# A decoder step on one core: the up products of the second MLP from seven block products in place of eight, in three of its four quarters, with sums of weights made in the first MLP

## The chip, the core and the metric

The kernel is one program on one core of a Trainium2 chip. TensorE (PE, its weight loads as PEld), VectorE (DVE), ScalarE (ACT), GpSimd (POOL) and SyncE (SP) run side by side, each through its own queue in order, and wait for each other on semaphores. The metric is device time of one execution in microseconds (us). Three runs of the kernel before are shown, and one more execution was profiled.

## What is computed

The reference is one step of a two-layer decoder over 512 prompt rows and 8 sample rows, 520 in all, width 1024. A pooling mixer, a first MLP, a sparse attention and a second MLP follow each other. The part that the change rewrites is the MLP, which both layers run with their own weights:

```python
D_MODEL = 1024
D_FF = 4 * D_MODEL

def rmsnorm(x, g):
    xf = x.astype(jnp.float32)
    y = xf * lax.rsqrt(jnp.mean(xf * xf, axis=-1, keepdims=True) + RMS_EPS)
    return (y * g.astype(jnp.float32)).astype(x.dtype)

def sq_relu_mlp(h, g, w_up, w_down):
    a = jax.nn.relu(rmsnorm(h, g) @ w_up)
    return (a * a) @ w_down
```

`w_up` is 1024 x 4096, `w_down` 4096 x 1024, all in 32-bit floats.

## The kernel before, in words

Everything is kept with the features on the 128 partitions: the residual `h` is 8 tiles (`CT`) of 128 x 520, and a weight unit is a 128 x 8 x 128 block, 512 KB: 8 tiles along the contraction for 128 output features. To keep the precision of 32 bits on TensorE, each operand is split into a high part (`hi`, a copy rounded to fp32r, made on ACT) and a low part (`lo`, the rest, made on DVE by a subtraction, `lo_of`, L200). A product is the sum of three: hi x hi, hi x lo, lo x hi. `gemm` (L231) therefore issues for a unit 8 tiles x 3 products x 2 halves of the 520 columns (`NH` = 260), which is 48 matmuls of 128 x 260.

An MLP (`mlp_jobs`, L695) goes in four quarters. A quarter has 8 up units (`up_post`, L705: evacuation from PSUM with relu and the norm on DVE, square on ACT, square and low part on DVE, into one of the tiles `at`) and then 8 down units that contract those 8 tiles and add into `h` (`down_post`, L716). The last down quarter of the second MLP (`last_quarter`, L745) goes by column halves, so that the first half's final norm runs beside the second half's products. In the first MLP (layer 0), between units, jobs of the compressed attention branch are filled in, by a table of 64 numbers (`FILLERS`, L42).

The order on every engine is written out by hand: `run` (L244) goes through a list of jobs. A job has loads (issued on SP's queue as `room` allows), a preparation (`prep`: the split of its weights, emitted two prepared jobs ahead), its matmuls (`pe`) and steps after them (`post`; the nth list entry is emitted n jobs later). A raw weight block lands in one of three buffers `wraw`; its split lands in one of two pairs `whi`, `wlo`. PSUM has two `mm` tiles and two `aux` tiles for the products. POOL issues no DMA in the first MLP and does nothing in the second but one multiplication at its end.

These lines carry most of it:

```python
for k, (xh, xl) in enumerate(xs):
    for wt, x in ((w.hi, xh), (w.hi, xl), (w.lo, xh)):
        for i in cols:
            TE.matmul(ps[0:m, i, 0:NH], wt[:, koff + k, 0:m], x[:, i * NH:(i + 1) * NH], ...

self.raw = wp.tile([P, 8, 128], F32, name="wraw", bufs=3)
nc.sync.dma_start(self.raw[:, 0:self.kt, 0:self.m], self.src)
```

Of the kernel before, what the change touches and what calls it, by code (L numbers as in the profile page):

```python
# [10 lines left out]
OP = mybir.AluOpType  # L11
# [127 lines left out]
class Job:  # L139
# [2 lines left out]

    after = None
# [6 lines left out]
def trunk(tc, a, o):  # L152
# [23 lines left out]
    hsave = pool("hd", space=bass.MemoryType.DRAM).tile([P, CT, NT], F32, name="hsave")  # L176
# [67 lines left out]
    def run(js, ahead=1, done=0):  # L244

        n = len(js)
        queue = {k: [(i, f) for i, j in enumerate(js) for c, f in j.loads if c == k] for k in room}
        issued = {k: 0 for k in room}

        def pump():  # L250
            for k in room:
                q = queue[k]
                while issued[k] < len(q) and room[k] > 0:
                    q[issued[k]][1]()
                    issued[k] += 1
                    room[k] -= 1

        with_prep = [i for i, j in enumerate(js) if j.prep]
        bars = [i for i, j in enumerate(js) if j.bar]

        def preps(i):

            nonlocal done
            while bars and bars[0] <= i:
                bars.pop(0)
            due = ahead - sum(k > i for k in with_prep[:done])
            for k in with_prep[done:done + due]:
                if bars and k > bars[0]:
                    break
                js[k].prep()  # L270
                done += 1
                for c, m in js[k].free_prep.items():
                    room[c] += m
                pump()

        late = {}
        pump()
        preps(-1)
        for i in range(n + 8):
# [10 lines left out]
            pump()  # L290
            if j.pe:
# [37 lines left out]
    def norm_job(emit=lambda: None):  # L329
        box = {}  # L330

        def pe():
            for i in range(2):
                box[i] = st["aux"]()
                TE.matmul(box[i][:, 0:NH], onesm, accn[:, i * NH:(i + 1) * NH], start=True, stop=True)  # L335

        def post():
            inv_rms(box)
            emit()

        return Job(pe=pe, post=post)
# [353 lines left out]
    def mlp_jobs(l, filler, done, before=lambda: None):  # L695
        ap, kind = {}, "w2" if l else "w"

        def open_a():
            ap["p"] = pool("ap")
            if l:  # L700
                pool("wz")

        at = {}

# [18 lines left out]
        js = []  # L723
        for q in range(4):
            for f in range(8):
                js.append(gemm_job(W(a["up"][l, 8 * q + f]), xpairs, up_post(8 * q + f), kind=kind))
                if not l and q in (1, 2):
                    js[-1].after = lambda x=("wink", "winv")[q - 1], b=f: S.dma_start(o[x][b], a_in[x][b])
                if q == f == 0:
                    js[-1].post.insert(0, None)  # L730
                    js[-1].after = lambda: (before(), open_a())
                    js.append(norm_job())
                js += filler()
            for ct in range(CT):
                xs = (lambda q=q: [(at[8 * q + k][:, 0], at[8 * q + k][:, 1]) for k in range(8)])
                if l and q == 3:
                    continue
                js.append(gemm_job(W(a["down"][l, q, ct]), xs, down_post(q, ct), kind=kind))
                js += filler()
        if l:  # L740
            js += last_quarter(xs)
        js.append(Job(hook=lambda: close(*["wz"] * l, "ap")))
        return js

    def last_quarter(xs):  # L745
# [1205 lines left out]
```

## Time and profile before

| what | value |
|---|---|
| three runs | 1391.57, 1390.76, 1391.56 us, median 1391.56 |
| the profiled execution | 1392.16 us, its span 1390.0 us |
| PE busy | 1345.2 us, 97% of the span, 10827 matmuls |
| PEld busy | 1261.3 us, 91% |
| DVE busy | 836.7 us, 60% |
| ACT busy | 570.8 us, 41% |
| POOL busy | 190.3 us, 14% |
| DMA | 189.52 MB, mean 136 GB/s |

The first MLP lies between about 150 and 590 us of the span, the second between about 1009 us and the end. A busy PE only says that matmuls overlap in the records: how long a unit takes is read from the distance between steps that follow each unit. An engine's idle time is listed with what ended it, and counts only where somebody waits for that engine.

### The profile page before, as it was taken

What the parts mean: (1) busy time and instruction counts of PE and PEld (TensorE: products, weight loads), DVE (VectorE), ACT (ScalarE), POOL (GpSimd) and SP (SyncE); (2) the same over time, 40 slices, a digit from 0 to 9 for tenths busy, and PEclk for the clock granted to TensorE, in tenths of its full rate; (3) what the DMA queues carried; (4) which work ended last, traced back from release to release, by engine and by line L of the source; (5) the groups of instructions that cost most, each with busy time, mean ns of one, the idle gap of its engine ahead of it and who ended that gap; (6) DMA issues with size and microseconds to landing.
All of it is one profiled execution on the core that took longest, in us unless ns stands there. A gap on an engine that the chain in (4) does not pass through costs nothing. (4 is left out here: it accounts for less than half of the span.)

```text
span 1390.0 us, 27557 instructions
## 1 busy us (share of the span) xinstructions
PE 1345.2 (97%) x10827; PEld 1261.3 (91%) x10827; DVE 836.7 (60%) x1307; ACT 570.8 (41%) x1012; POOL 190.3 (14%) x265
## 2 busy tenths in 40 slices
PE   7999999999999999999998999998999999999997
PEld 6788999999999999989996777667999999999996
DVE  2788766565565476556878887554554353453563
ACT  3655443333333243464445677563432222221231
POOL 0000000000000000012455764751000000000000
PEclk9999999999999999999999999999999999999999
DMA  7755244554455232339505675766223233322321
GB/s 261 224 153 185 77 136 137 167 165 139 139 172 161 76 107 77 98 131 231 142 26 177 187 207 185 215 204 193 92 87 94 91 94 95 96 92 91 92 91 62
DMA packets 110554, 189.52 MB, mean 136 GB/s; under 512 B 13641, under 2 KB 81482, under 8 KB 109786
## 3 DMA queue, kind: packets, MB, share of 16 engines
q1 hardware_dynamic: 102202, 166.65, 38.6%
q0 software_dynamic: 7168, 12.21, 3.6%
q10 hardware_dynamic: 1056, 8.92, 1.9%
q8 instruction: 85, 1.39, 0.4%
q14 instruction: 43, 0.35, 0.1%
HBM read 177.59 MB, written 16.43 MB: 140 GB/s over the span
## 5 line engine op out<-in xcount | busy, mean ns | idle before, releaser
L237 PE MATMUL mm<-xn,whi 128*128 128x260 f32 (+1 forms) x2784 | 450.0, 284 | 0.4 <-DVE xn L201 0.3
L237 PEld LDWEIGHTS mm<-xn,whi 128*128 128x128 f32 (+1 forms) x2784 | 383.1, 189 | 1.6 <-DVE xn L201 0.5
L201 DVE TENSOR_TENSOR wlo<-wraw,whi 128x1024 fp32r<-128x1024 f32 x163 | 200.6, 1231 | 257.5 <-ACT whi L221 257.2
L237 PE MATMUL mm<-at,whi 128*128 128x260 f32 x2048 | 332.6, 281 | 0.3 <-DVE at L201 0.3
L221 ACT ACTIVATE whi<-wraw 128x1024 fp32r<-128x1024 f32 x163 | 171.5, 1053 | 313.6 <-PE mm L237 257.1
L237 PEld LDWEIGHTS mm<-at,whi 128*128 128x128 f32 x2048 | 283.9, 188 | 1.0 <-DVE at L201 0.5
L237 PE MATMUL mm<-xn,wlo 128*128 128x260 f32 (+1 forms) x1392 | 281.1, 283 | 0.0
L237 PE MATMUL mm<-at,wlo 128*128 128x260 f32 x1024 | 215.9, 282 | 0.0
L237 PEld LDWEIGHTS mm<-xn,wlo 128*128 128x128 f32 (+1 forms) x1392 | 215.2, 188 | 0.0
L237 PEld LDWEIGHTS mm<-at,wlo 128*128 128x128 f32 x1024 | 161.4, 188 | 0.0
L201 DVE TENSOR_TENSOR clo<-craw,chi 128x512 fp32r<-128x512 f32 x128 | 85.3, 686 | 43.6 <-ACT chi L439 28.6
L710 ACT ACTIVATE at<-tmp 128x520 fp32r<-128x520 f32 x64 | 40.9, 639 | 143.2 <-DVE tmp L708 143.2
L1144 POOL TENSOR_TENSOR P<-P,sm 128x1024 f32<-128x1024 f32 (+1 forms) x64 | 81.9, 1290 | 3.8
L711 DVE TENSOR_TENSOR tmp<-tmp 128x520 f32<-128x520 f32 x64 | 44.8, 701 | 45.1 <-ACT at L710 45.1
L1129 ACT ACTIVATE P<-sc,sm 128x512 f32<-128x512 f32 (+3 forms) x128 | 66.0, 529 | 8.4 <-DVE sm L1117 8.2
L818 POOL MEMSET V2c<- 128x1024 f32 x1 | 1.0, 957 | 473.0 <-PE mm L237 473.0
L1244 PE MATMUL pt<-cst,P 128*128 128x128 f32 x320 | 53.0, 282 | 10.5 <-POOL P L1144 5.5
L789 POOL TENSOR_TENSOR h<-h,rn 128x260 f32<-128x260 f32 x2 | 1.9, 946 | 439.7 <-ACT rn L784 439.7
L1244 PEld LDWEIGHTS pt<-cst,P 128*128 128x128 f32 x320 | 37.3, 142 | 26.0 <-issue 6.8
L708 DVE SCALAR_TENSOR_TENSOR tmp<-mm,rn 128x520 f32<-128x520 f32 x64 | 44.5, 695 | 26.1 <-PE mm L237 21.6
L1117 DVE TENSOR_REDUCE sm<-sc 128x2 f32<-128x1024 f32 (+1 forms) x64 | 50.7, 815 | 13.2 <-PE sc L1090 8.8
L439 ACT ACTIVATE chi<-craw 128x512 fp32r<-128x512 f32 x64 | 37.0, 623 | 51.0 <-PE hid L451 35.4
(291 smaller groups left out, 1982.0 us busy)
## 6 DMA issues: line engine op xcount, KB each, us to landing
craw<-in_cc_dram SPq DMA_DIRECT2D x256, 128.0 KB
wraw<-in_up_dram SPq DMA_DIRECT2D x64, 512.0 KB
wraw<-in_down_dram SPq DMA_DIRECT2D x64, 512.0 KB
wraw<-in_selv_dram SPq DMA_DIRECT2D x62, 128.0 KB
wraw<-in_selk_dram SPq DMA_DIRECT2D x59, 128.0 KB
kvs<-in_selk_dram SPq DMA_DIRECT2D x53, 128.0 KB
kvs<-in_selv_dram SPq DMA_DIRECT2D x50, 128.0 KB
wraw<-in_wkv_dram SPq DMA_DIRECT2D x12, 512.0 KB
```

The source lines that it names most:

```text
L201: V.tensor_tensor(out, x, hi.bitcast(F32), op=OP.subtract)
L221: S.activation(hi, raw, AF.Copy)
L237: TE.matmul(ps[0:m, i, 0:NH], wt[:, koff + k, 0:m], x[:, i * NH:(i + 1) * NH], start=(k == 0 and wt is w.hi and x is xh), stop=(k == n - 1 ...
L439: S.activation(hv, src, AF.Copy)
L708: V.scalar_tensor_tensor(halves(r), view(ps), 0.0, halves(rn), op0=OP.max, op1=OP.mult)
L710: S.activation(t[:, 0], r, AF.Square)
L711: V.tensor_mul(r, r, r)
L789: G.tensor_tensor(h[:, ct, sl], h[:, ct, sl], rn[:, sl], op=OP.mult)
L1117: V.tensor_reduce(sm[:, c:c + 2], src, axis=AX.XY if len(src.shape) == 4 else AX.X, op=OP.max, negate=True)
L1129: S.activation(dst, src[:, b], AF.Exp, bias=sm[:, c:c + 1], accum_out=sm[:, m + c:m + c + 1])
L1144: G.tensor_tensor(x, x, sm[:, c:c + 2, None].to_broadcast(list(x.shape)), op=OP.mult)
L1244: TE.transpose(ps[:, 128 * x:128 * x + 128], ab["P", t, s, q][:, c:c + 128], ident)
```

## The change

**In the second MLP**, quarters 1 to 3 (of 0 to 3), the 8 up units become 4 pairs. A pair is a product of a 1024 x 256 weight block with the normed input. Weights and input are cut into 2 x 2 blocks (contraction in halves of 4 tiles; the pair's two units; the two column halves), and the block product is made with seven block products instead of eight, by sums of blocks (`seven_jobs`). Each block product is 4 tiles x 3 = 12 matmuls of 128 x 260 (`times`, L878 of the changed kernel), high products first, and is a job of its own: `pe1`, `pe6`, `pe5`, `pe7`, `pe2`, `pe3`, `pe4`. `pe1` and `pe2` add into one `mm` tile (`a`), `pe7` and `pe4` into the other (`e`), `pe6`, `pe5`, `pe3` take the `aux` tiles (`b`, `c`, `d`).

- The input's sums: in quarter 0 the normed input is written once to a tile in the place of the old `h` (`normed`, 8 operations on DVE), and `moving` makes the seven blocks with their high and low parts during the first seven down units of quarter 0 (4 subtractions of 128 x 1040 and 7 low parts on DVE, 7 copies of 128 x 1040 on ACT), into `X`.
- The weights' sums: 12 tensors `sums` in DRAM, 1 MB each, made in the first MLP. 48 steps (`sum_steps`) each load 256 KB (two DMAs on POOL's queue), make four 128 x 128 operations in place on DVE, and store 256 KB (one DMA on POOL's queue). A step's load is emitted two of its slots ahead of its sums; 50 of the 64 units carry a slot.
- A pair loads four blocks on SP's queue: `A1` (512 KB of the weights), `S24` and `S13` (512 KB of sums each, in pieces of 1 KB), `A22` (256 KB). `A1`, `S24`, `S13` are split into a ring of four places: the two `whi`, `wlo` pairs and two more in the old `h` (`ring`).
- The recombination is five additions of 128 x 260 on DVE (`u2`, `u4`, `c22`, `c12`, `c21`) and a copy and two relus of 128 x 260 on ACT (`keep1`, `c11`, `relu12`); then a relu and four squares of 128 x 520 on ACT and two low parts on DVE for the two tiles `at`.
- `Job` gets `before`: steps emitted ahead of the job's matmuls. Every step of a pair has its slot there. The splits of the next pair's `A1`, `S24`, `S13` are emitted ahead of this pair's `pe2`, `pe3`, `pe4`. For the first pair of a quarter they are emitted behind the matmuls of the last down unit (`entry`).
- The last down quarter's weights keep the two `wp` pairs for the first two units and six places of a pool `wz`, which is opened only after `X` is closed. A `bar` keeps the second unit's split from being emitted ahead of the first unit's matmuls. The right half of the last pair's tiles is made ahead of the second unit (`sv["right"]`).

```diff
-            for f in range(8):
+            if l and q:
+                for i in range(4):
+                    js += seven_jobs(q, i, at, ap, js[-3 if i else -1:])
+            for f in range(8 if not (l and q) else 0):
...
+                if l and 1 <= f <= 4:
+                    units[-1].post[0] = lambda x=units[-1].post[0], ct=2 * f - 2: (x(), [normed(c) for c in (ct, ct + 1)])
...
+                if l and not q and ct < 7:
+                    js[-1].post[0] = lambda x=js[-1].post[0], ct=ct: (x(), moving(ct))
...
+            js.append(Job(hook=open_z))
+            n = len(js)
             js += last_quarter(xs)
+            js[n].bar, js[n + 1].before = True, sv["right"]
+        else:
+            steps = [sum_steps(n) for n in range(48)]
...
+            for j, old, new in zip(due, [()] * 2 + steps, [x[:1] for x in steps] + [()] * 2):
+                j.post.append(lambda fs=(*old[1:], *new[:1]): [f() for f in fs])
...
+        def load():
+            box["w"] = pools["pf"][1].tile([P, 2, 2, 128], F32, name="sraw", bufs=2)
+            src = a["up"][1, 8 + 2 * pair:10 + 2 * pair].rearrange("f p (h j) n -> p f h j n", h=2)[:, :, :, j]
+            for f in range(2):
+                G.dma_start(box["w"][:, f], src[:, f])
+
+        def add():
+            w = box["w"]
+            V.tensor_tensor(w[:, 1, 1], w[:, 1, 0], w[:, 1, 1], op=OP.add)
+            V.tensor_tensor(w[:, 1, 0], w[:, 0, 0], w[:, 1, 0], op=OP.subtract)
+            V.tensor_tensor(w[:, 0, 0], w[:, 1, 1], w[:, 0, 0], op=OP.subtract)
+            V.tensor_tensor(w[:, 0, 1], w[:, 0, 1], w[:, 0, 0], op=OP.subtract)
+
+        def store():
+            G.dma_start(sums[pair][:, 4 * j:4 * j + 4], box["w"].rearrange("p f h n -> p (f h) n"))
...
+        def times(w, k0, x, out, first=True, last=True):
+            for n, (wt, k, part) in enumerate([(w.hi, k, part) for k in range(4) for part in (0, 1)] + [(w.lo, k, 0) for k in range(4)]):
+                TE.matmul(out, wt[:, k0 + w.step * k], sv["X"][:, x, part, k], start=first and n == 0, stop=last and n == 11,
+                          skip_group_check=True)
...
+        tail = [[c21, lambda: squares(0)], [relu2, lambda: low(0)], [lambda: squares(1)], [lambda: low(1)]]
...
+        slots = [[S13.low], [keep1, A22.high], [u2, A22.low], [u4], [c22], [c11], [c12, relu12]]
...
+        first = [[A1.high], [A1.low, S24.high], [S13.high, S24.low]]
+        js = []
+        for k, (pe, w) in enumerate([(pe1, A1), (pe6, S24), (pe5, S13), (pe7, None), (pe2, None), (pe3, None), (pe4, A22)]):
+            js.append(Job(pe=pe, loads=[("w2", w.load)] if w else (), bar=i == 3 and k == 4))
+            js[-1].before = slots[k]
...
-        ws = [W(a["down"][1, 3, ct], home=lambda: (pools["wz"][1], CT)) for ct in range(CT)]
+        ws = [W(a["down"][1, 3, ct], **({} if ct < 2 else dict(home=lambda: (pools["wz"][1], CT - 2)))) for ct in range(CT)]
```

How the order moves, first on PE, second MLP, quarter 3 before: the end of a down unit and the start of the first up unit (`xn` is the input, `at` the squared tiles).

```order
L237 MATMUL mm_15418<-at_14900,wlo_15356 128x260 x2
L237 MATMUL mm_15418<-at_14961,whi_15355 128x260 x4
L237 MATMUL mm_15418<-at_14961,wlo_15356 128x260 x2
L237 MATMUL mm_15418<-at_15022,whi_15355 128x260 x4
L237 MATMUL mm_15418<-at_15022,wlo_15356 128x260 x2
L237 MATMUL mm_15474<-xn_12155,whi_15411 128x260 x4
L237 MATMUL mm_15474<-xn_12155,wlo_15412 128x260 x2
```

And the second pair of quarter 1 in the changed kernel (`h_14017` is the part of the ring in the old `h`, `dhi`, `dlo` the split of `A22`):

```order
L878 MATMUL mm_14156<-X_13102,whi_14098 128x260 x8
L878 MATMUL mm_14156<-X_13102,wlo_14099 128x260 x4
L878 MATMUL aux_14178<-X_13102,whi_14115 128x260 x8
L878 MATMUL aux_14178<-X_13102,wlo_14116 128x260 x4
L878 MATMUL aux_14197<-X_13102,h_14017 128x260 x12
L878 MATMUL mm_14215<-X_13102,h_14017 128x260 x12
L878 MATMUL mm_14156<-X_13102,whi_14098 128x260 x8
L878 MATMUL mm_14156<-X_13102,wlo_14099 128x260 x4
L878 MATMUL aux_14249<-X_13102,whi_14115 128x260 x8
L878 MATMUL aux_14249<-X_13102,wlo_14116 128x260 x4
L878 MATMUL mm_14215<-X_13102,dhi_14175 128x260 x8
L878 MATMUL mm_14215<-X_13102,dlo_14176 128x260 x4
```

Two units had 96 matmuls, alternately high and low; the pair has 84, in seven groups of 12, each with its low parts last.

On ACT, an up quarter of the second MLP before:

```order
L221 ACTIVATE whi_14587<-wraw_14423 128x1024
L710 ACTIVATE at_14595<-tmp_14593 128x520
L221 ACTIVATE whi_14648<-wraw_14479 128x1024
L710 ACTIVATE at_14656<-tmp_14654 128x520
L221 ACTIVATE whi_14709<-wraw_14535 128x1024
```

and one period of a pair in quarter 2 of the changed kernel (`tmp` are the two result tiles, `p1` the copy of `a`):

```order
L864 ACTIVATE h_14017<-wraw_15238 128x1024
L924 ACTIVATE tmp_15337<-mm_15265 128x260
L864 ACTIVATE h_14017<-wraw_15258 128x1024
L864 ACTIVATE whi_15371<-wraw_15278 128x1024
L932 ACTIVATE tmp_15337<-tmp_15337 128x260
L946 ACTIVATE at_15392<-tmp_15337 128x520
L947 ACTIVATE tmp_15337<-tmp_15337 128x520
L940 ACTIVATE tmp_15338<-tmp_15338 128x520
L909 ACTIVATE p1_15413<-mm_15396 128x260
L864 ACTIVATE dhi_15415<-wraw_15319 128x512
L946 ACTIVATE at_15431<-tmp_15338 128x520
L947 ACTIVATE tmp_15338<-tmp_15338 128x520
```

Four operations for two units became twelve: the next pair's three splits stand between `c11` (L924) and `relu12` (L932), and the tiles of a pair are finished in the next pair's time.

On DVE in the first MLP, around one step of the weights' sums (clo, dlo and the tmp rows belong to a filled-in job):

```order
+L203 TENSOR_TENSOR wlo<-wraw,whi 128x1024
+L722 TENSOR_TENSOR h<-h,mm 128x520
+L551 COPY cV<-aux 127x256
+L792 TENSOR_TENSOR sraw<-sraw 128x128
+L793 TENSOR_TENSOR sraw<-sraw 128x128
+L794 TENSOR_TENSOR sraw<-sraw 128x128
+L795 TENSOR_TENSOR sraw<-sraw 128x128
+L203 TENSOR_TENSOR clo<-craw,chi 128x8x4x16
+L479 TENSOR_TENSOR tmp<-craw 128x8x2x16
+L203 TENSOR_TENSOR clo<-craw,chi 128x8x4x16
+L479 TENSOR_TENSOR tmp<-craw 128x8x2x16
+L203 TENSOR_TENSOR dlo<-tmp,dhi 128x512
```

The four operations of a step stand behind a unit's evacuation and ahead of the next split.

## Rows read from the trace of the kernel before

**Rows 1.** The page: busy time of the engines, and PE and DVE in 40 slices of the span (tenths).

```profile
PE 1345.2 (97%) x10827; PEld 1261.3 (91%) x10827; DVE 836.7 (60%) x1307; ACT 570.8 (41%) x1012; POOL 190.3 (14%) x265
PE   7999999999999999999998999998999999999997
DVE  2788766565565476556878887554554353453563
```

**Rows 2.** The chain that ended last, in order of time: start, length, what. The two longest pieces.

```profile
1015.98 315.86 PE mm L237 x2640
1334.76 23.50 PE mm L237 x194
```

**Rows 3.** Windows of the span: for each the length, then busy us and (instructions) of PE, PEld, DVE, ACT and POOL, the granted clock of TensorE, the DMA engines' share and GB/s. In order: the start, the first MLP, the last part of the key and value stage, three quarters and more of the second MLP.

```profile
0.00:100.00 100.00, 89.47 (x408) 73.18 (x409) 61.97 (x99) 50.91 (x79) 2.29 (x10) 1.00 0.68 211
150.00:590.00 440.00, 440.00 (x3664) 435.33 (x3664) 267.99 (x402) 163.06 (x230) 1.13 (x3) 1.00 0.41 127
650.00:700.00 50.00, 49.83 (x416) 49.00 (x415) 40.76 (x67) 24.68 (x38) 20.33 (x30) 1.00 0.69 150
1011.00:1331.00 320.00, 320.00 (x2674) 319.88 (x2673) 147.85 (x177) 83.23 (x94) 0.00 (x0) 1.00 0.30 93
```

**Rows 4.** Waits in the second MLP (1005 us to the end): who waited for whom, total us, times, longest. The two longest of the engines that split weights, and all that PE had for an operand of a unit.

```profile
ACT whi L221 <- PE mm L237: 173.4, 53, 4.7
DVE wlo L201 <- ACT whi L221: 152.9, 61, 3.9
...
PE mm L237 <- DVE at L201: 0.3, 1, 0.3
```

**Rows 5.** DVE's timeline: the steps after the first up unit of quarter 1 of the second MLP and after its first down unit, 8 units later (start, length).

```profile
1109.84 0.69 DVE L708 SCALAR_TENSOR_TENSOR tmp<-mm,rn 128x520 f32<-128x520 f32 x1
...
1155.94 0.69 DVE L718 TENSOR_TENSOR h<-h,mm 128x520 f32<-128x520 f32 x1
```

**Rows 6.** Groups by shape in the second MLP: busy us, mean ns of one, idle before.

```profile
L201 DVE TENSOR_TENSOR wlo<-wraw,whi 128x1024 fp32r<-128x1024 f32 x64 | 78.4, 1225 | 152.9 <-ACT whi L221 152.9
L221 ACT ACTIVATE whi<-wraw 128x1024 fp32r<-128x1024 f32 x63 | 66.7, 1059 | 176.5 <-PE mm L237 173.4 <-issue 3.1
L201 DVE TENSOR_TENSOR at<-tmp,at 128x520 fp32r<-128x520 f32 x32 | 22.4, 700 | 1.1
L710 ACT ACTIVATE at<-tmp 128x520 fp32r<-128x520 f32 x32 | 20.5, 639 | 62.2 <-DVE tmp L708 62.2
L760 DVE TENSOR_TENSOR h<-h,mm 128x260 f32<-128x260 f32 x16 | 6.8, 422 | 13.5 <-PE mm L237 13.5
L765 ACT ACTIVATE tmp<-h 128x260 f32<-128x260 f32 x14 | 5.9, 422 | 28.1 <-DVE h L760 28.1
L346 DVE SCALAR_TENSOR_TENSOR xn<-h,gv,xn 128x520 fp32r<-128x520 f32 x2 | 1.5, 760 | 1.6 <-ACT xn L345 1.6
```

**Rows 7.** Groups by shape in the first MLP (150 to 590 us), the same columns.

```profile
L201 DVE TENSOR_TENSOR clo<-craw,chi 128x512 fp32r<-128x512 f32 x62 | 42.5, 685 | 12.9 <-ACT chi L473 11.1 <-DMA craw<-in_cc_dram 1.8
L475 DVE TENSOR_TENSOR tmp<-craw 128x256 f32<-128x256 f32 x62 | 25.9, 418 | 0.0
L473 ACT ACTIVATE chi<-craw 128x512 fp32r<-128x512 f32 x62 | 35.7, 622 | 39.3 <-PE hid L494 32.5 <-issue 3.5 <-DMA craw<-in_cc_dram 3.1
```

**Rows 8.** The same view in the attention (750 to 950 us), the one 128 x 128 sum of two tensors on DVE.

```profile
L1114 DVE TENSOR_TENSOR accn<-sc,sm 128x128 f32<-128x128 f32 x14 | 4.1, 292 | 0.5
```

**Rows 9.** Timelines of DVE and ACT: a low part in the second MLP, whose end frees the raw buffer for the one load then due, and a copy on ACT whose raw data had just landed.

```profile
1154.80 1.23 DVE L201 TENSOR_TENSOR wlo<-wraw,whi 128x1024 fp32r<-128x1024 f32 x1 [1.76 <-ACT whi L221]
...
228.06 1.15 ACT L473 ACTIVATE chi<-craw 128x512 fp32r<-128x512 f32 x2 [3.53 <-issue]
```

**Rows 10.** Windows of half a microsecond, columns as in rows 3: the load that follows that low part (no other is under way), and the end of the loads that the copy on ACT took.

```profile
1156.50:1157.00 0.50, 0.50 (x6) 0.50 (x6) 0.13 (x1) 0.00 (x0) 0.00 (x0) 1.00 0.00 0
1157.00:1157.50 0.50, 0.50 (x6) 0.50 (x5) 0.00 (x0) 0.00 (x0) 0.00 (x0) 1.00 0.82 131
1158.50:1159.00 0.50, 0.50 (x7) 0.50 (x6) 0.00 (x0) 0.00 (x0) 0.00 (x0) 1.00 0.74 303
1159.00:1159.50 0.50, 0.50 (x6) 0.50 (x6) 0.00 (x0) 0.08 (x1) 0.00 (x0) 1.00 0.17 66
...
227.50:228.00 0.50, 0.50 (x6) 0.50 (x6) 0.00 (x0) 0.00 (x0) 0.00 (x0) 1.00 0.18 33
```

**Rows 11.** DVE's timeline in quarter 0 of the first MLP: two evacuations with a filled-in job between them, and a low part with the evacuation behind it, which waited for PE.

```profile
153.08 0.69 DVE L708 SCALAR_TENSOR_TENSOR tmp<-mm,rn 128x520 f32<-128x520 f32 x1
160.64 0.69 DVE L708 SCALAR_TENSOR_TENSOR tmp<-mm,rn 128x520 f32<-128x520 f32 x1
...
179.26 1.22 DVE L201 TENSOR_TENSOR wlo<-wraw,whi 128x1024 fp32r<-128x1024 f32 x1
182.27 0.70 DVE L708 SCALAR_TENSOR_TENSOR tmp<-mm,rn 128x520 f32<-128x520 f32 x1 [1.78 <-PE mm L237]
```

**Rows 12.** DMAs issued by POOL in the key and value stage: the tile view of `out_kv_dram` (260 KB each; ns of an issue, then us to landing) and of `Kd` (128 KB each, SBUF to SBUF).

```profile
L869 POOL DMA_DIRECT2D out_kv_dram<-kt x12: 542/565/1022, 607.6 to 677.0; - x12
DMA to landing us min/median/max: 2.5/3.1/5.3
...
DMA to landing us min/median/max: 2.4/5.3/6.6
```

More of the change, by code (lines that the diff above doesn't have):

```diff
@@ L139 @@
 class Job:
-    after = None
+    after, before = None, ()
     def __init__(self, pe=None, post=None, prep=None, loads=(), hook=None, free_prep=None, free_pe=None, bar=False):
@@ L175, in trunk @@
     h = con.tile([P, CT, NT], F32, name="h")
-    hsave = pool("hd", space=bass.MemoryType.DRAM).tile([P, CT, NT], F32, name="hsave")
+    hd = pool("hd", space=bass.MemoryType.DRAM)
+    hsave = hd.tile([P, CT, NT], F32, name="hsave")
+    sums = [hd.tile([P, 16, 128], F32, name=f"sums{i}") for i in range(12)]
     ptab = con.tile([1, 2 * DB * NPAGE], I32, name="ptab")
@@ L290, in run @@
             pump()
+            for f in j.before:
+                f()
             if j.pe:
@@ L700, in open_a @@
             if l:
-                pool("wz")
+                open_x()
         at = {}
@@ L731, in mlp_jobs @@
                     js[-1].after = lambda: (before(), open_a())
+                    units.append(js[-1])
                     js.append(norm_job())
+                else:
+                    units.append(js[-1])
+                if l and 1 <= f <= 4:
+                    units[-1].post[0] = lambda x=units[-1].post[0], ct=2 * f - 2: (x(), [normed(c) for c in (ct, ct + 1)])
                 js += filler()
@@ L738, in mlp_jobs @@
                 js.append(gemm_job(W(a["down"][l, q, ct]), xs, down_post(q, ct), kind=kind))
+                js[-1].bar = bool(l and q and not ct)
+                units.append(js[-1])
+                if l and not q and ct < 7:
+                    js[-1].post[0] = lambda x=js[-1].post[0], ct=ct: (x(), moving(ct))
                 js += filler()
         if l:
+            js.append(Job(hook=open_z))
+            n = len(js)
             js += last_quarter(xs)
+            js[n].bar, js[n + 1].before = True, sv["right"]
+        else:
+            steps = [sum_steps(n) for n in range(48)]
+            short = [i for i in range(2, 64) if not FILLERS[i]]
+            left = {i for k, i in enumerate(short) if 12 * (k + 1) // len(short) > 12 * k // len(short)}
+            due = [u for i, u in enumerate(units) if i > 1 and i not in left]
+            assert len(due) == 50
+            for j, old, new in zip(due, [()] * 2 + steps, [x[:1] for x in steps] + [()] * 2):
+                j.post.append(lambda fs=(*old[1:], *new[:1]): [f() for f in fs])
@@ L742, in mlp_jobs, with sum_steps @@
         js.append(Job(hook=lambda: close(*["wz"] * l, "ap")))
         return js
+    def sum_steps(n):
+        pair, j = divmod(n, 4)
+        box = {}
+        def load():
[11 more added lines that the diff above has]
+            G.dma_start(sums[pair][:, 4 * j:4 * j + 4], box["w"].rearrange("p f h n -> p (f h) n"))
+        return load, add, store
@@ new lines, in trunk, with open_x, open_z, normed @@
+    sv = {}
+    def open_x():
+        xs = pool("xs")
+        sv["X"] = xs.tile([P, 7, 2, 4, NH], F32R, name="X")
+        sv["xt"] = con.tile([P, CT, NT], F32, name="h")
+        sv["n"] = 0
+    def open_z():
+        close("xs")
+        pool("wz")
+    def normed(ct):
+        V.scalar_tensor_tensor(sv["xt"][:, ct], h[:, ct], gv[:, 3, ct:ct + 1], rn, op0=OP.mult, op1=OP.mult)
+    def moving(i):
+        x = sv["xt"].rearrange("p (k c) (h n) -> p k h c n", k=2, h=2)
+        B = [[x[:, k, i] for i in range(2)] for k in range(2)]
+        if i == 3:
+            V.tensor_tensor(B[0][0], B[0][1], B[0][0], op=OP.subtract)
+        elif i == 4:
+            V.tensor_tensor(B[0][1], B[1][1], B[0][1], op=OP.subtract)
+        elif i == 5:
+            V.tensor_tensor(B[1][1], B[1][1], B[0][0], op=OP.subtract)
+        elif i == 6:
+            V.tensor_tensor(B[1][0], B[1][0], B[1][1], op=OP.subtract)
+        src = (B[0][0], B[1][0], B[1][1], B[0][0], B[0][1], B[1][1], B[1][0])[i]
+        S.activation(sv["X"][:, i, 0], src, AF.Copy)
+        lo_of(sv["X"][:, i, 1], src, sv["X"][:, i, 0])
```

109 lines of the change are left out of this document (108 added, 1 removed).

## The prediction

> **What bounds the kernel now.** I read the page first, then the chain that ended last, then windows by stage, then the waits of the two MLPs, and last single steps. The page gives PE 97% of the span and DVE 60% [rows 1]; the slices show no long hole on PE. The chain [rows 2] is nearly one piece of PE through the second MLP, 315.86 us without another engine in it. The windows say the same by stage: PE is busy in all 440 us of the first MLP and all 320 us of the second that were cut out, at a granted clock of 1.00, the 2.4 GHz level, while DVE is at 61% and 46%, ACT at 37% and 26% [rows 3]. In the second MLP ACT waits for PE to give a weight buffer back, 53 times, and DVE waits for ACT; PE waited for an operand of a unit once, for 0.3 us [rows 4]. So in both MLPs time is the number of matmuls times their distance, and other engines count only once they make PE wait.
>
> The distance is not in a matmul's own duration, which overlaps the next. From the step after the first up unit to the step after the first down unit, 8 units later, 46.10 us pass [rows 5]: 5.76 us a unit, and with 48 matmuls **0.120 us each**.
>
> **The change, part by part.** The sum is against the profiled execution, 1392.16 us; the median of the runs shown lies 0.6 us lower.
>
> *Matmuls.* A pair has 84 matmuls of the same shape for 96. 12 x 0.120 = 1.44 us, and 12 pairs give **-17.3 us**. They lie on the path [rows 2]. Nothing shorter comes of it: the other operations that go were already hidden. A pair now takes 84 x 0.120 = 10.08 us, a job of 12 matmuls 1.44 us.
>
> *Does a pair's work fit into 10.08 us?* ACT: three splits at 1.059, one of 128 x 512 at 0.622 [rows 7], five passes of 128 x 520 at 0.639, three of 128 x 260 at 0.422 [rows 6]; 3.18 + 0.62 + 3.20 + 1.27 = 8.3 us, 82%. DVE: three low parts at 1.225, one of 128 x 512 at 0.685, five additions at 0.422, two low parts at 0.700; 3.68 + 0.69 + 2.11 + 1.40 = 7.9 us, 78%. Both fit, but engines in order can still block. I laid the slots out with PE at 1.44 us a job and 0.1 us from engine to engine. From the end of `pe3` (8.64) ACT runs `S13` high, `relu12`, two squares, relu, `keep1`, `A22` high, two squares and the next `A1` high without a hole until 15.5, 5.4 us into the next pair; `c11` needs `pe2`, which ends at 7.2. So ACT has a cushion of 1.8 us in each pair, and none of the seven groups waits: `A1`'s high part is ready 4.6 us before `pe1` and its low part 2.5 us, and `u2` has emptied its `aux` tile 3.8 us before `pe3` takes it.
>
> *The loads.* They are the tight part, since four loads a pair turn over in three raw buffers. In that layout `S13` may take longest 4.6 us from the low part that frees its buffer to its own split, `A1` 4.1 us (5.9 with the cushion), `A22` 5.0 us, `S24` 6.0 us. A load alone: the low part ends at 1156.03 [rows 9], the DMA engines are at work from about 1157.1 to 1159.2 [rows 10], 3.2 us. A split on ACT began 0.4 us after its loads' activity had died away [rows 9, 10], so **3.6 to 3.7 us** to use. That leaves 0.4 to 1 us. SP's queue holds nothing but these loads until the outputs, so a load delays only the next load. The traffic is 1.84 MB in 10.08 us, 182 GB/s, where the start of the kernel carried 211 GB/s with the engines at 68% [rows 3]. Loads overlap by about a microsecond now, so some will be later: below 0; above, 0.5 us a pair, 6 us. I take **+1 us**, near the lone load, which is the nearer row.
>
> *The weights' sums in the first MLP.* 192 operations of 128 x 128; the nearest row is 0.292 us [rows 8], 1.17 us a step and 56 us in all. DVE has 440 - 268 = 172 us idle there and would go from 61% to 74% [rows 3]. PE takes weights two preparations ahead, so a delay of DVE below that lead costs nothing. The cover is thin where filled-in jobs follow each other: between two evacuations with such a job 7.56 us pass [rows 11], of which DVE works about 6.2 (three passes of 128 x 520 at 0.70, a low part 1.2, the job's two low parts and two differences and its own low part 2.9 [rows 6, 7]). Another low part ended 1.8 us before PE had finished the unit ahead [rows 11]; one step fits into that, two do not. Bounds: nothing, and 56 us if none were hidden. Since PE had no wait at all there, the lower end is nearer; I take **+2 us**.
>
> The step's DMAs: each store waits for its sums and the load behind it for the store, both on POOL's queue, with nothing else in it. Issues take 0.57 us each and land in 3.1 us in the median, 5.3 at most, beside DVE at 82% (40.76 of 50 us) [rows 3, 12]: store, load and issues make about 8 us. The load is wanted two slots on, 11.5 us or more. So DVE should not stop at its sums. POOL's DMAs are the place where a rule speaks against the change. The Trainium skill, "SBUF — State Buffer", section "SBUF: two separate sides", says that a DMA issued by POOL starves while DVE runs an operation in a mode that takes both port pairs, and names copies; its section "Who interferes with whom" grants a sum of two tensors no such mode. By it, landings would stretch wherever DVE runs such copies, and not beside sums; no run here sets the two apart. The landings of 3.1 us beside a busy DVE speak for no stretching. The traffic there goes from 127 by 57 (25 MB in 440 us) to 184 GB/s.
>
> *Edges of the second MLP.* Eight `normed` operations (0.76 each [rows 6]) and seven blocks of `moving` fall into quarter 0, where DVE has over 2 us free in a unit of 5.76: nothing. At the last quarter the second unit's weights may be split only behind the first unit's matmuls are emitted, behind the last pair's left half: ACT gets to it at 1.8 us after that unit's start, its high part is made by 2.9 and its low part by 4.1; the first unit lasts 24 x 0.120 = 2.9 us, and the second's third matmul, at 3.1, wants the low part. **+1 us.**
>
> The sum: 1392.2 - 17.3 + 1 + 2 + 1 = 1378.9; less 0.6 for the median, **1378 us**.
>
> **The rivals.** *All hidden:* loads and sums cost nothing; for it, PE's clean record [rows 3, 4], against it, the thin cover of [rows 11]. 1391.6 - 17.3 + 1 = 1375 us. *Sums gate the first MLP:* DVE, not PE, sets the pace where filled-in jobs stand close. If a tenth to a half of the 56 us shows, 6 to 28 us, it is 1382 to 1404. Against it, 172 us idle; for it, [rows 11]. *Slower, by late loads in the second MLP:* past 4.6 us every microsecond of a load is a microsecond of each pair, since the ring of three turns no faster; 12 us for each. At 6.0 us the gain is gone, at 6.6 us the time is 1391.6 - 17.3 + 24 + 1 = 1399. It decides from 6.0 us on. For it, three loads in flight and the pieces of 1 KB; 128 KB between partitions took up to 6.6 us [rows 12]. Against it, the lone load's 3.7. *POOL's DMAs starve:* a step whose store and load both take 6.6 us [rows 12] needs 14.9 us with three issues, 3.4 over the 11.5; DVE has (172 - 56) / 64 = 1.8 us idle a unit after the sums, so 1.6 us shows in each of 48 steps, 77 us: 1455. It needs the longest landing every time, where the median is 3.1 to 5.3. This is what the Trainium skill's rule above would do if DVE's sums counted under it. *The change gains nothing in PE:* block products with another weight block for each matmul could come at a longer distance. Against it, weights were loaded for every matmul already (10827 for 10827 [rows 1]). 1391.
>
> **How the numbers follow.** No change can be told from one below 0.2%, 2.8 us: the lines are 1388.8 and 1394.3. My forecast, the gain less a few microseconds (1376 to 1384), has 0.50, all hidden 0.20. Sums gating the first MLP 0.14: 0.07 still faster than 1388.8, 0.04 near no change, 0.03 slower. Late loads 0.11: 0.05 faster, 0.02 near no change, 0.04 slower. Starving DMAs 0.02, no gain on PE 0.03. Faster: 0.50 + 0.20 + 0.07 + 0.05 = 0.82. Same: 0.04 + 0.02 + 0.03 = 0.09. Slower: 0.03 + 0.04 + 0.02 = 0.09. The range leaves out the slower cases and the top of the gating ones: 1373.5 (nothing costs anything, and the matmuls come a touch closer) to 1389.
>
> **What would show it.** Right: 84 matmuls a pair, 10.1 us from one pair's `u2` to the next; ACT idle ahead of `c11` and waiting for PE, not for a DMA; PE without waits from 150 to 590 us, that stage still 440 us long; the last quarter's second unit waiting about 1 us for its low part. Wrong: ACT's wait ahead of a split put down to a DMA of `wraw`, and pairs of 10.5 us or more; PE waiting for a low part in the first MLP, or DVE waiting for `sraw`; the distance of matmuls in a pair above 0.120 us.

## The result, and the profile after

The changed kernel took **1380.62 us** (median of four runs, 1377.52 to 1383.09), the kernel before 1391.16 beside it: a ratio of 0.9925, 95% interval 0.9903 to 0.9947, or 10.5 us less (7.4 to 13.5). The forecast was 1378, with 1373.5 to 1389 as its range. The profiled execution took 1383.09 us with a span of 1381.3, against 1392.16 and 1390.0 before.

The page of the changed kernel (busy us, share of the span, instructions), which answers [rows 1]:

```profile
PE 1331.8 (96%) x10683; PEld 1245.9 (90%) x10683; DVE 916.3 (66%) x1556; ACT 627.6 (45%) x1120; POOL 284.1 (21%) x409
```

PE is still the bound; DVE, ACT and POOL have more to do. The chain that ended last, from the second MLP on, answers [rows 2, 5]:

```profile
1021.17 86.08 PE mm L239 x720
1107.25 1.43 PE mm L878 x12
...
1147.49 45.78 PE mm L239 x384
1193.27 1.43 PE mm L878 x12
...
1233.52 45.78 PE mm L239 x384
1279.30 1.43 PE mm L878 x12
...
1323.49 1.22 DVE wlo L203
...
1330.17 18.17 PE mm L239 x144
1348.34 0.44 PE aux L1016 x2
```

The four pairs of quarter 1 last from 1107.25 to 1147.49: 40.24 us, 10.06 a pair, where eight units took 46.10. Quarters 2 and 3 are the same. Then the chain leaves PE: between 1319 and 1330 us it runs through ACT and DVE.

Two windows, columns as in [rows 3]: the first MLP, and the pairs of quarter 2.

```profile
150.00:590.00 440.00, 438.61 (x3633) 432.33 (x3633) 314.11 (x587) 160.99 (x228) 91.02 (x139) 1.00 0.58 181
...
1193.00:1233.00 40.00, 40.00 (x337) 40.00 (x336) 27.10 (x41) 24.92 (x41) 0.00 (x0) 1.00 0.58 179
```

In the pairs PE has no hole. In the first MLP it has 1.4 us of idle time, where it had none (by the cuts below that stage is 3.3 us longer, so the records show less than half of it as idle), and DVE is at 71% for 61%.

To see where the 8.7 us of the two spans went, I cut each profiled execution at the same instructions: the copy on ACT at 150 us, the last addition to `h` of the first MLP, the sum for the norm ahead of the second MLP, the first such sum in the last quarter. All kernels of the experiments are in the table, us:

| kernel | first MLP | K/V and attention | second MLP | last half quarter and end |
|---|---|---|---|---|
| before | 436.64 | 427.83 | 343.15 | 31.91 |
| the change | 439.96 | 429.81 | 328.05 | 33.12 |
| sums_alone | 439.13 | 427.41 | 343.16 | 33.17 |
| seven_alone | 435.50 | 427.43 | 328.04 | 31.87 |
| early_last | 438.67 | 425.86 | 326.91 | 33.19 |
| pool_adds | 436.72 | 428.45 | 328.05 | 33.53 |
| both | 437.27 | 426.00 | 326.91 | 33.49 |
| both_order | 437.78 | 427.54 | 325.27 | 33.52 |
| both_again | 437.94 | 429.92 | 327.08 | 33.57 |
| order_again | 436.59 | 426.42 | 325.27 | 33.55 |
| s13_half | 439.43 | 427.44 | 337.93 | 33.13 |
| s13_twice | 438.05 | 427.40 | 346.19 | 33.14 |
| loads_alone | 436.30 | 429.09 | 343.17 | 31.00 |
| adds_stores | 436.13 | 427.33 | 343.17 | 31.07 |

The change against before: +3.3 in the first MLP, +2.0, -15.1, +1.2 and -0.1 ahead of the first cut. The second column has a spread of 4 us though no kernel touches that stage: its 2.0 us are not the change's (early_last, which has the change's instructions there, has 425.86). That spread goes, for the most part, with TensorE's granted clock. Between 590 and 750 us of the span its mean is 0.98 in the three kernels with the shortest second column (early_last, both, order_again) and 0.96 in the three with the longest (the change, loads_alone, both_again); 1.00 would be the 2.4 GHz level throughout. One run doesn't fit: pool_adds, with 0.98 and 428.45 us. The windows of both and both_again, which are one kernel run twice:

```profile
590.00:750.00 160.00, 148.79 (x1280) 142.87 (x1279) 114.82 (x188) 81.88 (x141) 60.84 (x98) 0.98 0.50 136
...
590.00:750.00 160.00, 150.53 (x1210) 146.02 (x1208) 112.03 (x171) 79.71 (x131) 58.97 (x96) 0.96 0.50 141
```

The third column repeats to 0.2 us and is the place to read terms of the second MLP; the first differs by up to 1.9 us between executions of like work (438.05 to 439.96).

### The profile page after: what moved, and what is told of

Its sections match the earlier page's. It is cut to its first block, busy times and chain, and to the rows that moved or that the text cites. A ratio compares the mean times of both kernels' runs of the same rounds, so it can differ in the third digit from the quotient of the medians.

```text
span 1381.3 us, 28013 instructions
## 1 busy us (share of the span) xinstructions
PE 1331.8 (96%) x10683; PEld 1245.9 (90%) x10683; DVE 916.3 (66%) x1556; ACT 627.6 (45%) x1120; POOL 284.1 (21%) x409
## 5 line engine op out<-in xcount | busy, mean ns | idle before, releaser
L239 PE MATMUL mm<-xn,whi 128*128 128x260 f32 (+1 forms) x2016 | 327.3, 285 | 0.4 <-DVE xn L203 0.3
L203 DVE TENSOR_TENSOR wlo<-wraw,whi 128x1024 fp32r<-128x1024 f32 x157 | 193.0, 1230 | 158.9 <-ACT whi L223 156.4
L239 PEld LDWEIGHTS mm<-xn,whi 128*128 128x128 f32 (+1 forms) x2016 | 278.6, 189 | 1.6 <-DVE xn L203 0.5
L223 ACT ACTIVATE whi<-wraw 128x1024 fp32r<-128x1024 f32 x139 | 145.8, 1051 | 207.1 <-PE mm L239 140.1
L239 PE MATMUL mm<-xn,wlo 128*128 128x260 f32 (+1 forms) x1008 | 204.2, 284 | 0.0
L239 PEld LDWEIGHTS mm<-xn,wlo 128*128 128x128 f32 (+1 forms) x1008 | 156.1, 189 | 0.4 <-DVE wlo L203 0.2
L788 POOL DMA_DIRECT2D sraw<-in_up_dram x96 | 67.7, 709 | 185.2 <-DMA sums<-sraw 158.5
L798 POOL DMA_DIRECT2D sums<-sraw x48 | 26.8, 558 | 208.2 <-DVE sraw L795 201.6
L714 ACT ACTIVATE at<-tmp 128x520 fp32r<-128x520 f32 x40 | 25.6, 639 | 89.0 <-DVE tmp L712 89.0
L1481 PE MATMUL pt<-cst,P 128*128 128x128 f32 x320 | 53.2, 283 | 10.5 <-DVE kt L1261 4.7
L481 ACT ACTIVATE dhi<-tmp 128x512 fp32r<-128x512 f32 x32 | 20.2, 633 | 93.3 <-DVE tmp L479 93.3
```

Source lines behind the costliest of these rows:

```text
L203: V.tensor_tensor(out, x, hi.bitcast(F32), op=OP.subtract)
L223: S.activation(hi, raw, AF.Copy)
L714: S.activation(t[:, 0], r, AF.Square)
L788: G.dma_start(box["w"][:, f], src[:, f])
L798: G.dma_start(sums[pair][:, 4 * j:4 * j + 4], box["w"].rearrange("p f h n -> p (f h) n"))
L1481: TE.transpose(ps[:, 128 * x:128 * x + 128], ab["P", t, s, q][:, c:c + 128], ident)
```

## The experiments

**The sums alone.** Into the kernel before:

```
+            steps = [sum_steps(n) for n in range(48)]
...
+                j.post.append(lambda fs=(*old[1:], *new[:1]): [f() for f in fs])
```

> The kernel before with the 48 sum steps of the first MLP added in the change's own places; the second MLP is that of before and never reads the sums. Theory A (the sums' price is small and lies in the first MLP, where DVE, in order, does its four operations ahead of a filled-in job's): the last accumulation of the first MLP ends 3.3 us later than in the kernel before, as in the trace of the change, and the time is 1391.2 + 3.3 = 1394.5 us. Theory A2: the 1.9 us that the change loses between there and the second MLP (K/V and attention) come of the sums too: 1396.4. Rival B (prediction's term): +2, 1393.2. Rival C (the sums are free, the loss comes of something else in the change): 1391.2.

1394.71 us beside 1390.14, ratio 1.003 (1.0017 to 1.0042): 4.6 us, 2.4 to 5.8. The first MLP is 2.5 us longer and the end 1.3; the K/V stage and attention are not, so A2 falls. C falls; A holds in its place, with a size between its 3.3 and B's 2; the end was in no theory.

**The seven products alone.**

```
-            for j, old, new in zip(due, [()] * 2 + steps, [x[:1] for x in steps] + [()] * 2):
-                j.post.append(lambda fs=(*old[1:], *new[:1]): [f() for f in fs])
-        s_ = sums[4 * (q - 1) + i].rearrange("p (j g s) n -> p g j (s n)", g=2, s=2)
+        s_ = a["up"][1, 8 * q + i // 2 * 4:][0:4].rearrange("f p (g s) n -> p g f (s n)", s=2)[:, i % 2 * 2:][:, 0:2]
```

> The change without the sum steps: the two loads of sums in each pair take other blocks of the same weights, in the same pieces of 1 KB, so three quarters of the up products are of other matrices; amounts, shapes and order are those of the change. Theory A: the first MLP is that of before again, 1380.6 - 3.3 = 1377.3 us; with theory A2 1375.4. Rival B (prediction's sizes): 1380.6 - 2 = 1378.6. Rival C (sums free): 1380.6. In all of them a pair lasts 10.06 us as in the change; were it longer, the place that the sums are loaded from would matter.

1374.48 us, ratio 0.9888 (0.987 to 0.9906), 15.7 us less. The second MLP takes 328.04, the change's own 328.05: where the sums are loaded from makes no difference. The first MLP is whole again:

```profile
150.00:590.00 440.00, 440.00 (x3659) 435.06 (x3658) 267.93 (x402) 163.55 (x231) 1.13 (x3) 1.00 0.42 129
```

A's 1377.3 is 2.8 us too high, B and C more. 1.3 us of that are the end, which no theory had; the rest is within the spread of the first two columns. (A2's 1375.4 is nearer, but A2 fell with the run before.)

**The additions on POOL.**

```
-            V.tensor_tensor(w[:, 1, 1], w[:, 1, 0], w[:, 1, 1], op=OP.add)
+            G.tensor_tensor(w[:, 1, 1], w[:, 1, 0], w[:, 1, 1], op=OP.add)
...
```

> The change with the 192 additions of weights on POOL instead of DVE; loads, stores and their traffic stay. Theory A (DVE's order costs the 3.3 us of the first MLP): DVE is rid of 56 us, the waits for the filled-in jobs' operands go, 1380.6 - 3.3 = 1377.3 us. Rival B (the traffic or the issues cost it): the waits stay, 1380.6. Rival C (POOL's operations slow DVE's down, since both work in SBUF at once, or last so long that the sums fall behind): 1381 to 1386, with DVE's means of the first MLP up.

1378.1 us, ratio 0.9916 (0.9899 to 0.9932). The traffic is the same, and PE's idle time in that stage falls from 1.4 to 0.3 us:

```profile
150.00:590.00 440.00, 439.70 (x3658) 434.65 (x3658) 283.69 (x403) 162.74 (x230) 207.57 (x324) 1.00 0.58 182
```

By time the kernel is not to be told from the change. A's place is right, and B falls for the larger part. C is half right: DVE has the instructions of the kernel before and 15.7 us more of busy time (267.99 there [rows 3]). Not all of the price goes: the five kernels with the additions on POOL have 436.59 to 437.94 us in the first MLP, mean 437.3, which is 1.8 below the five with whole steps on DVE and 1.1 above the four without whole steps.

**Loads alone, additions and stores alone,** each in the kernel before. In the second the operands lie in a resident tile:

```
+            w, z = box["w"], cst[:, 0:256].rearrange("p (z n) -> p z n", z=2)
+            V.tensor_tensor(w[:, 1, 1], z[:, 0], z[:, 1], op=OP.add)
...
```

> The kernel before with the 96 loads of the sum steps on POOL's queue alone, 12.6 MB: no additions, no stores. In the profiles so far the time from the last store's issue to the end of the span is 4.2 us in the two kernels without sum steps and 5.4 us in all ten with them, whoever adds, and no record stands in it. Theory A (DVE's order costs the 2 to 3.3 us of the first MLP): the first MLP as in the kernel before, 436 to 437 us between the marks used so far. Theory E1 (the 1.2 us at the end come of more DMAs on POOL's queue): end at 4.6 to 5.4 us. Theory E2 (they come of the stores to memory of its own): end at 4.2. Time by A and E1 1391.5 to 1392, by A and E2 1390.5.

> The kernel before with the additions of the sum steps, on operands that lie in SBUF anyway, and the 48 stores, 12.6 MB written; no loads. Theory A: the first MLP 2 to 3 us longer than in the kernel before, as with whole sum steps, 438.5 to 439.5 between the marks. Rival B (loads or the total traffic cost it): 436 to 437. Theory E1: end between 4.2 and 5.4 us, by the number of DMAs; theory E2: 5.4. Time by A 1393.5 to 1394.5, by B 1391.

Neither costs anything that stands out from the spread: 1390.61 us (ratio 0.9993, 0.9981 to 1.0004) and 1389.45 (0.9994, 0.9982 to 1.0005); 436.30 and 436.13 us in the first MLP. For the loads theory A had said so; for the additions it had said 2 to 3 us, and it missed. Place by place, each loses a little against the kernel before: the additions 0.6 us between 182 and 206 us, the loads 0.8 between 226 and 247. DVE's timeline in that kernel, one step and the low part behind it:

```profile
187.74 0.28 DVE L770 TENSOR_TENSOR sraw<-cst 128x128 f32<-128x128 f32 x1
187.94 0.29 DVE L771 TENSOR_TENSOR sraw<-cst 128x128 f32<-128x128 f32 x1
188.15 0.28 DVE L772 TENSOR_TENSOR sraw<-cst 128x128 f32<-128x128 f32 x1
188.35 0.29 DVE L773 TENSOR_TENSOR sraw<-cst 128x128 f32<-128x128 f32 x1
188.55 1.22 DVE L203 TENSOR_TENSOR wlo<-wraw,whi 128x1024 fp32r<-128x1024 f32 x1
```

A step takes 0.81 us there, the additions 0.20 apart. The change's, on the same engine:

```profile
184.56 0.28 DVE L792 TENSOR_TENSOR sraw<-sraw 128x128 f32<-128x128 f32 x1
184.88 0.29 DVE L793 TENSOR_TENSOR sraw<-sraw 128x128 f32<-128x128 f32 x1
185.20 0.29 DVE L794 TENSOR_TENSOR sraw<-sraw 128x128 f32<-128x128 f32 x1
185.53 0.29 DVE L795 TENSOR_TENSOR sraw<-sraw 128x128 f32<-128x128 f32 x1
185.83 0.69 DVE L203 TENSOR_TENSOR clo<-craw,chi 128x512 fp32r<-128x512 f32 x1
...
189.71 0.41 DVE L506 TENSOR_TENSOR tmp<-tmp,hid 128x256 f32<-128x256 f32 x1
190.23 0.42 DVE L507 TENSOR_TENSOR tmp<-tmp,hid 128x256 f32<-128x256 f32 x1
190.57 0.28 DVE L792 TENSOR_TENSOR sraw<-sraw 128x128 f32<-128x128 f32 x1
```

In place, each addition touches what the one before it touched: the second overwrites an operand of the first, the third reads the first's result, the fourth the third's. In the trace each of these three carries a wait on DVE's own semaphore, and the additions from the resident tile carry none. In place they stand 0.32 apart and a step takes 1.27 us. Two steps embrace a filled-in job here, and PE waits for that job's operands, the `tmp` of 189.71 among them. The waits of PE and of its weight loads in the first MLP (total us, times, longest):

```profile
PE hid L498 <- DVE tmp L506: 0.6, 1, 0.6
...
PEld hid L498 <- ACT whi L223: 1.2, 2, 0.8
```

Instruction by instruction against the kernel before, the change loses 1.5 us between 168 and 206 us and 1.4 between 370 and 449; in between DVE comes up to 2.2 us later than that and catches up without PE. The first place repeats: from 182 to 206 us each of the five kernels with whole steps on DVE loses 1.8 us; at the second they lose 0.7 to 2.0. So the price lies in DVE's order, at two crowded places. But the run without loads also took away the dependence, and two waits of DVE for a load (1.8 us in the change): which of these lets the price vanish isn't settled.

**The last quarter's second unit split early.**

```
-            js[n].bar, js[n + 1].before = True, sv["right"]
+            js[n + 1].before = sv["right"]
```

> The change without the bar on the last quarter's first unit: the second unit's weights are split right behind the first's, while the last pair's products still run; the four right-half passes stay where they are. Theory A (the last quarter loses 2.4 us since the second unit's low part comes 0.85 us late and, with ACT and DVE then behind, the fourth unit waits 1.0 us for a PSUM tile): both waits go, first down matmul to the norm's sum 26.6 us instead of 29.0, and 1380.6 - 2.4 = 1378.2 us. Theory B (only the first wait goes): 1379.8. Rival C (the split, now ahead of the last pair's relu, holds that back, and PE waits for the left halves of at): 1380 to 1382.

1379.09 us, ratio 0.9924 (0.9909 to 0.9939), not to be told from the change by time; the second MLP is 1.14 us shorter, 326.91. That is B: one wait goes, the other stays. PE's one wait there is now the fourth unit's:

```profile
1323.50 0.48 PE L239 MATMUL mm<-at,whi 128*128 128x260 f32 x2 [0.87 <-DVE h L997]
```

DVE's timeline in the change at this place:

```profile
1322.35 2.36 DVE L203 TENSOR_TENSOR wlo<-wraw,whi 128x1024 fp32r<-128x1024 f32 x2 [0.52 <-ACT whi L223]
1324.63 0.42 DVE L997 TENSOR_TENSOR h<-h,mm 128x260 f32<-128x260 f32 x1
1326.30 0.43 DVE L203 TENSOR_TENSOR at<-tmp,at 128x260 fp32r<-128x260 f32 x1 [1.25 <-ACT tmp L947]
1327.52 0.43 DVE L203 TENSOR_TENSOR at<-tmp,at 128x260 fp32r<-128x260 f32 x1 [0.79 <-ACT tmp L947]
1328.46 1.23 DVE L203 TENSOR_TENSOR wlo<-wraw,whi 128x1024 fp32r<-128x1024 f32 x1 [0.52 <-ACT whi L223]
1329.61 0.42 DVE L997 TENSOR_TENSOR h<-h,mm 128x260 f32<-128x260 f32 x1
```

and PE's, its two waits:

```profile
1323.63 0.39 PE L239 MATMUL mm<-at,wlo 128*128 128x260 f32 x1 [0.75 <-DVE wlo L203]
...
1330.17 0.48 PE L239 MATMUL mm<-at,whi 128*128 128x260 f32 x2 [0.76 <-DVE h L997]
```

The second unit ended at 1326.4 and its addition to `h` began at 1329.61, behind the right half's low parts and a weight's; the fourth unit wants that PSUM tile.

**Both repairs, and the right half's passes moved.** Both kernels have the additions on POOL and no `bar`. The second has this in place of the `before`:

```
             def post():
+                right = sv["right"] if not ct and not i else []
+                for f in right[:3]:
+                    f()
                 V.tensor_add(h[:, ct, sl], h[:, ct, sl], box["ps"][:, i, 0:NH])
+                for f in right[3:]:
+                    f()
```

> The change with both repairs tried so far: the sums' additions on POOL, and no bar on the last quarter's first unit. Theory A (the first MLP's price is DVE's order, the second unit's late low part costs 1.1 us, and the two are in different places): both gains add up, 1378.1 - 1.1 = 1377.0 us, first MLP within 0.2 us of the kernel before. Rival (POOL's 207 us of additions are not free elsewhere, or the two hide each other): 1378 or more.

> The same with the right-half passes of the last pair moved: squares and low part of one product ahead of the first unit's addition to h, those of the other between that addition and its square on ACT. Theory A (the fourth unit waits 0.9 us for a PSUM tile since the second unit's addition to h stands on DVE behind a low part whose split on ACT stands behind the right-half passes, which wait for that addition's square): the wait goes, 0.9 us less than with both repairs, 1376.1. Rival (the wait only moves, to the third unit's tile, which the first unit's later addition frees): as with both repairs, 1377.0, with PE waiting at the third unit.

1374.78 us (ratio 0.9893, 0.9874 to 0.9912) and 1376.43 (0.9901, 0.9884 to 0.9919). The chain of the second shows 216 matmuls without a wait, from the first of the last quarter to its sum:

```profile
1313.52 26.02 PE mm L239 x216
1339.54 0.44 PE aux L1019 x2
```

From the first matmul on (1313.35) that is 26.2 us; it is 28.96 in the change. The second MLP is 1.64 us shorter than with both repairs, more than the 0.9 expected: a late tile also cost each of the five units behind it 0.1 to 0.2 us. The medians stood the other way, so both ran again:

> The kernel with both repairs once more, beside the one with the right-half passes moved. In the stretch from the norm ahead of the second MLP to the last quarter's first sum the moved passes took 1.65 us less, while the medians of five runs stood 1.65 us the other way, each with intervals of some 2.5 us to either side. Theory A (the stretch decides, the rest is spread of the attention and of the outputs): this one 1375 to 1377 us, the other 1 to 2 us less. Rival (the moved passes cost elsewhere what they gain): this one 1 us or more below the other again.

> The kernel with both repairs and the right-half passes moved, once more. Theory A: 1374 to 1375 us, 1 to 2 us below the one with both repairs alone. Rival (the move costs elsewhere what it gains): 1376 or more, not below the other.

1376.42 (0.989, 0.9872 to 0.9908) and 1375.68 (0.9894, 0.9877 to 0.9911). The stage repeats to 0.2 us (327.08, 325.27), the times don't tell the two apart: the attention's spread is larger. Both kernels are about 15 us faster than before and 4 to 6 below the change's median.

**A later load in each pair.**

```
+                    if self.late:
+                        nc.sync.dma_start(self.raw.rearrange("p (j s) n -> p j (s n)", s=2)[:, 0:2], self.src[:, 0:2])
```

> The change with half of S13's load (256 KB) loaded a second time into the same place, behind the first, in each of the 12 pairs: the load takes about 1.9 us longer (a lone 512 KB load is at work for 2.1 us, and a second issue waits for the first to land). In the trace of the change S13 comes 5.1 us after its buffer was freed, ACT waits up to 0.6 us for it, and still has 2.0 us of idle time ahead of c11. Theory A (lateness of a load is taken from that idle time first): 1.9 us fit into 2.0, 0 to 0.3 us a pair, 1380.6 to 1384 us. Rival B (prediction's rule, a pair lengthens by each us past 4.6, from the lone load's 3.7): 5.6 us, 1.0 us a pair, 1392.6. Rival C (the same from the measured 5.1): 7.0 us, 2.4 a pair, 1409.

> The same with all of S13 loaded a second time: about 3.6 us longer. Theory A: 3.6 - 2.0 = 1.6 us a pair too late for c11, and with it the next pair's A1; 12 x 1.6 = 19, 1400 us; pairs of 11.7 us, ACT without idle time ahead of c11. Rival B: 7.3 us, 2.7 a pair, 1413. Rival C: 8.7 us, 4.1 a pair, 1430. Rival D (the ring of three buffers turns freely and only DMA time counts, 14.4 MB more at some 160 GB/s elsewhere hidden): 1380.6.

1392.52 us (ratio 1.0019, 1.0004 to 1.0033) and 1399.38 (1.0067, 1.0046 to 1.0087). By the second MLP, +9.9 and +18.1 us over the change: 0.82 and 1.51 a pair in the mean of the twelve. Theory A had 0 to 0.3 and 1.6: right for the second, too low for the first. B had 1.0 and 2.7: near for the first, far too high for the second. C and D fall (the second kernel moves 6.3 MB more than the change, not D's 14.4). ACT's timeline with half of the load repeated, in the last pair:

```profile
1316.29 1.06 ACT L868 ACTIVATE whi<-wraw 128x1024 fp32r<-128x1024 f32 x1 [3.99 <-DMA wraw<-sums]
...
1321.42 1.05 ACT L223 ACTIVATE whi<-wraw 128x1024 fp32r<-128x1024 f32 x1
1322.37 0.37 ACT L930 ACTIVATE tmp<-mm 128x260 f32<-128x260 f32 x1
```

ACT waits 4.0 us for the sums and then comes to `c11` (L930) without idle time: the cushion is used up. So late loads do what the rival said, by an estimate from about 1 us later than now on (1.9 us more cost 0.82), and unevenly: with all of it repeated, the pairs of quarter 2 take 10.1, 11.4, 13.8 and 11.1 us, and the first pair of each quarter keeps its 10.06 in both kernels.

## Why the prediction was right, by its steps

*Matmuls, -17.3:* right. Pairs of 10.06 us for 11.52 give -17.5; the distance stayed 0.120. The whole stage shows -15.1, since the last quarter lies in it.

*Does a pair's work fit:* right. ACT's waits in the pairs and downs of 1100 to 1320 us:

```profile
ACT tmp L924 <- PE mm L878: 23.7, 12, 3.9
...
ACT whi L864 <- DMA wraw<-sums: 5.5, 7, 1.6
...
ACT whi L864 <- DMA wraw<-in_up_dram: 3.2, 2, 2.2
```

Ahead of each of the 12 `c11` ACT has idle time, 2.0 us in the mean (0.6 to 3.9), for the 1.8 laid out.

*The loads, +1:* too high, 0. They are later than I took them to be: in the last pair `S13`'s buffer was free at 1303.40 and its split began at 1308.55, 5.1 us where a lone load takes 3.7, and beyond the 4.6 that the layout allowed; ACT waited 0.6 us for it. The cushion took that, which the step had counted for `A1` and not for `S13`. The rival's price (one for one past 4.6) was too steep: with half of the load repeated `S13` took 6.6 us in the last pair, for which the rival said 1399, and the time was 1392.5.

*The sums in the first MLP, +2:* 3.3 in the profiled execution. The five kernels with whole steps on DVE have 438.05 to 439.96 us, mean 439.05; the four without whole steps (before, seven_alone, loads_alone, adds_stores), mean 436.14: **2.9 us**. A step was worked out at four times 0.292, 1.17 us; in place it takes up to 1.27. The place, two steps about a filled-in job, is the one that the step had named. *The POOL queue:* nearly right: DVE was not to stop at its sums, and waited twice for a load, 1.8 us. So two of the prediction's signs of being wrong showed, small: this one, and PE waiting for a low part in the first MLP, 0.2 us. The landings of the change in the first MLP, from issue, us:

```profile
sraw<-in_up_dram POOLq DMA_DIRECT2D x92, 128.0 KB, 3.3
sums<-sraw POOLq DMA_DIRECT2D x47, 256.0 KB, 3.4
```

Beside DVE at 71% they land as they did in [rows 12]. The Trainium skill's grant ("SBUF — State Buffer", "Who interferes with whom"), that a sum of two tensors starves no such DMA, agrees with these 3.3 us.

*The last quarter, +1:* the failed step. Its times were right: ACT came 1.9 us after the unit's start, the high part was made at 2.95, the low part at 4.2, and PE came 1.0 us late. This wait is worth 1.1 us, as the kernel without the `bar` shows. What the step left out is a second wait, for which it put down nothing: the right half's passes stand on ACT and DVE ahead of the second unit's addition to `h`, which frees the PSUM tile of the fourth unit. PE waited 0.9 us there, and the units behind lost 0.7 more. The late split is not its cause: it stays with the split early, and goes with the passes moved (1.6 us). The same 216 matmuls took 26.6 us before and 28.96 in the change: +2.4.

*What the sum lacked:* 1.2 us at the end of the span, which lie in POOL's closing drain (last section). Altogether -17.5 + 0 + 2.9 + 2.4 + 1.2 = -11, for -13.3 forecast and -10.5 measured. The terms that were too small come to 3.5 us; that the 1 us put down for the loads, which cost nothing, made up for a part of them is luck.

## What to carry to other kernels

A term for a late operand covers one wait. Work that is put into a short unit on engines that work in order has a second price: follow it up to the evacuations behind it and the buffers that they free. Where DVE has 39% idle time in a stage, small steps still cost where two of them meet a dense stretch. On an idle engine they cost less (1.8 of 2.9 us came back); putting them behind the stretch was not tried. Repairing both places gave 4 to 6 us of the 7 that the change had lost.

## What the runs showed of the hardware

DVE slows down beside POOL's additions, but only with both operands in SBUF. In the first MLP (busy us, mean ns, idle before), the addition to `h` before, then three groups with the additions on POOL:

```profile
L718 DVE TENSOR_TENSOR h<-h,mm 128x520 f32<-128x520 f32 x32 | 22.2, 693 | 30.8 <-PE mm L237 30.8
...
L203 DVE TENSOR_TENSOR clo<-craw,chi 128x512 fp32r<-128x512 f32 x62 | 46.8, 755 | 12.4 <-ACT chi L477 10.5 <-DMA craw<-in_cc_dram 1.8
L479 DVE TENSOR_TENSOR tmp<-craw 128x256 f32<-128x256 f32 x62 | 31.3, 505 | 0.0
...
L722 DVE TENSOR_TENSOR h<-h,mm 128x520 f32<-128x520 f32 x32 | 22.1, 692 | 26.9 <-PE mm L239 26.9
```

`clo` took 685 ns and `tmp` 418 [rows 7]; the addition to `h`, one operand of which is in PSUM, has 692 as it had 693. One by one it is the same: the `tmp` that POOL's additions cover by more than half took 679 ns (18 of them), the others 434; the `clo` 897 (14) and 714; the additions to `h` 691 (11) and 693. The Trainium skill, same section, says that a DVE instruction with two inputs in SBUF contends with a POOL instruction that reads SBUF; these means agree.

From the last store's issue to the end of the span 4.2 us pass in the kernels without sum steps, 5.5 in those with whole steps on DVE, 5.8 with the additions on POOL, and 3.3 with loads alone or with additions and stores alone. The views of busy time list nothing there, but the trace has the closing instructions of each engine: POOL's longest `DRAIN` begins 3.7 us before that issue ends in every kernel, and its length differs (ns, min, median, max; before, then the change):

```profile
L1937 POOLq DRAIN  x3: 51/107/7027, 1382.1 to 1389.7; - x3
...
L2174 POOLq DRAIN  x3: 51/103/8330, 1372.2 to 1381.1; - x3
```

The other engines wait for it: 1.30 us more is the price at the end. With loads alone it lasts 5.80 us, with additions and stores alone 3.43, and then SP, done 2.5 us after the issue, is the last. Since 48, 96 and 144 more DMAs of POOL give 3.4, 5.8 and 8.3 us and none more gives 7.0, their number alone doesn't order it: why it lasts that long stays open.
